# Even attention with its score tiles spread over the head, and its linear stages reordered

## The chip, the cores and the metric

The kernel runs on one core of one Trainium2 chip. The time is device microseconds for one execution, the median of three timed runs.

A core has five engines that run their own instruction queues side by side: TensorE (PE), which multiplies matrices and transposes; VectorE (DVE); ScalarE (ACT); GpSimd (POOL); and SyncE (SP), which here only starts DMAs. Results of PE go to PSUM, which has eight banks of 128 x 512 floats. PE's clock is either at its full level or at half of it; the profile gives the mean granted clock of a stretch as a share of the full one.

## What is computed

One step of a two-layer backbone on 128 prompt tokens and 512 sample tokens, all in 32-bit floats. Cut to what the change touches, the even layer is:

```
h   = rmsnorm(x) * (1 + scale) + shift
u   = h @ w_in                       # cq, ckv, kr, gate_a, q_b, k_b, v_b, gate_b
q   = rmsnorm(cq) @ w_uq             # 8 heads: 64 plain + 32 rotary columns
kv  = rmsnorm(ckv) @ w_ukv           # keys and values of the 8 MLA heads
o_a = softmax(q k^T) v * silu(gate_a)
o_b = softmax(q_b k_b^T) v_b * silu(gate_b)   # 8 heads, 2 key/value heads
x   = x + gate * (concat(o_a, o_b) @ w_out)
```

Sample tokens read 128 cached tokens and themselves (640 keys); prompt tokens read only the 128 prompt tokens. The odd layer has the same frame around an mLSTM (forward and backward, with a carried state) and a differential attention.

## The kernel before

Activations stand as 640 columns: 128 of the prompt, 512 of the sample. Nearly every product is computed as three passes over a high and a low part of both operands (`mm3`), the parts being made by a cast on ScalarE (`whi`, L76) and a subtraction (`wlo`, L77) for each weight piece. A scheduler orders each engine's instructions by a simulated timeline, with the order of the program as priority; within the even attention `pe_order` ties PE's instructions to the order in which the program issues them. `issue_after(x)` puts the instructions of a block behind x on x's engine.

**Linear stages of the even layer** (`even_linear`). Query lora and rotary key (e_wA), then ckv, k_b and v_b (e_wB), then the MLA queries in two halves (uq), values (ukvV, copied to `Va` by DVE at L559), keys (ukvK, copied to `kn` by ScalarE), and last q_b (e_wC) with its norm and rotation `evC` on DVE. Then `even_prep` lays out key tiles `Ka` and `kp`, the queries and keys of heads 0 and 1 are prepared, and `even_gates` multiplies the gates and applies silu (`silu_from`: a tanh on ScalarE, L127, and two DVE lines, L128 and L129, the second writing `og`).

**Even attention** (`attention`). Sixteen heads: 0 to 7 are the MLA heads, 8 to 15 the grouped ones. A head has four score tiles of 128 queries x 640 keys. `scores(h, i)` issues one: PE writes it into one of two score buffers (`s2`, two banks each); DVE takes the maximum (L628); ScalarE exponentiates it with the sum (L631); DVE inverts the sum (L634); GpSimd multiplies (L641). Three passes make an MLA tile, two a grouped one. `head_T(k)` transposes key block k of the head's four tiles (L648) into one of two `t1` banks, and ScalarE or DVE copies it to `pT` (L653, L651). `head_PV` multiplies the five blocks with the values, the value run (L659), into the one bank `o`; DVE multiplies that by the gate (L747). One iteration for head h issues, on PE, in this order: block 0 of h; tile 1 of h+1; block 1; tile 2; the transposes of the queries of h+2 (`prep[1]`, one call for two heads in the grouped part); block 2; tile 3; blocks 3 and 4; tile 0 of h+2; the value run of h; and `side(h)`, which holds the matmuls of the odd layer's modulation, later of the even gate. `prep[0]` casts the keys of h+2 (`kh` on DVE, L788) and subtracts (`kl` on GpSimd, L789). `split_psum` writes the query's upper part on ScalarE (L339) and the lower part on DVE (L340); in the grouped part these are L802 and L803.

The prompt's scores are computed four heads at a time by `prompt_quad`, in steps that `stage` advances: 0 prepares, 1 computes scores (L672) in a score buffer of `s2`, the maximum (L674), four exponentials `pp` (L678) and a product; 2 transposes; 3 multiplies with the values.

From head 12 on `op_load` fetches and splits output-projection weights (cast on ScalarE, subtraction on GpSimd), and in head 15 `ada_gate_row` sums the gate's parts, adds the bias (`grow`, L248) and sends the row to DRAM, from where `ada_gate_bc` reads it for the output projection.

**Odd layer.** `odd_linear` runs four projections (o_wK, o_wQ, o_wV1, o_wVM); `mlstm_gates`, a chain of scans on DVE with a few transposes, is issued after the first. In `mlstm_head`, for each of five blocks t, PE computes the value products `pv` (L1508) and then the product with the carried state `it`, which ScalarE scales into `nd` (L1518) and DVE adds (L1520). A `pacer` fills the gaps with matmuls of other projections, placed behind the instruction in `self.mark`.

Of the kernel before, what the change touches and what calls it, by code (L numbers as in the profile page):

```python
# [37 lines left out]
class K:  # L38
# [84 lines left out]
    def silu_from(self, out, src, shape, pool, other=None):  # L123

        nc = self.nc
# [4 lines left out]
        if other is not None:  # L130
            nc.vector.tensor_tensor(out=out, in0=out, in1=other, op=ALU.mult)
# [106 lines left out]
    def ada_gate_row(self, L, pool, tag, bufs):  # L238
# [103 lines left out]
    def even_linear(self, E, EM, H, L, ps):  # L342
# [198 lines left out]

        for hf in range(2):
# [11 lines left out]
        for t in range(6):  # L554
# [4 lines left out]
            nc.vector.tensor_copy(Va[:, t, :], acc)  # L559
# [12 lines left out]

        self.qb = E.tile([128, 5, 512], F32, tag="qb", name="qb", bufs=1)

        def evC(t, acc):
            q = self.qb[:, t]
            nc.scalar.copy(q, acc)
            qv = q.rearrange("p (h w) -> p h w", h=8)
            r = self.rsqrt(self.sumsq(q, 8, 64), 8, 64)
            nc.vector.tensor_tensor(out=qv, in0=qv, in1=r[:, :, None].to_broadcast([128, 8, 64]), op=ALU.mult)  # L580
            nc.vector.tensor_tensor(out=qv, in0=qv, in1=self.rows[:, None, R_GQ:R_GQ + 64].to_broadcast([128, 8, 64]),
                                    op=ALU.mult)
            if t:
                self.rope(qv, qv, *ropeB(t), 8, 64, L)

        self.lin_tok([(A["e_wC"][i], 2) for i in range(4)], 512, Hh, Hl, range(5), evC, ps)

# [3 lines left out]
    def even_gates(self, H, L, ps):  # L591
        Hh, Hl, A = self.Hh, self.Hl, self.A
        self.og = self.st.tile([128, 8, 640], F32, tag="ogx", name="og", bufs=1)
        for m in range(8):
            acc = self.lin_feat(A["e_wG"][m], Hh, Hl, ps)
            for j in range(2):
                self.silu_from(self.og[:, m, j * 320:j * 320 + 320], acc[j], [128, 320], L)
# [39 lines left out]
    def head_scores(self, T, ps, passes, i):  # L637
# [3 lines left out]
        self.nc.gpsimd.tensor_tensor(out=p, in0=p, in1=rs.to_broadcast([128, 640]), op=ALU.mult)  # L641
# [21 lines left out]
    def prompt_quad(self, T, ps, prep, V, cols, m):  # L663
# [4 lines left out]
        s = ps.tile([128, 2, 512], F32, tag="s2", name="sp", bufs=2)[:, 0]  # L668
# [1016 lines left out]
```

## Time and profile before

| | |
|---|---|
| median of three runs | 885.71 us (885.25 to 886.45) |
| the profiled execution | 888.68 us, its span 886.9 us |
| mean granted PE clock | 0.989 |
| busy of the span: PE, DVE, ACT, POOL | 839.8, 540.8, 416.9, 258.5 us |

The span runs from the first instruction to the last; the rest of an execution's time lies around it. The even layer's linear stages and gates take the span up to about 209 us, the even attention the stretch to 386.6, where the output projection begins. Busy times of the engines overlap, so they do not add up to the span. A busy PE is not a PE at its peak, since the profile models where a pipelined matmul ends. A wait is idle time of an engine before an instruction, put down to what released it.

### The profile page before, as it was taken

What the parts mean: (1) busy time and instruction counts of PE and PEld (TensorE: products, weight loads), DVE (VectorE), ACT (ScalarE), POOL (GpSimd) and SP (SyncE); (2) the same over time, 40 slices, a digit from 0 to 9 for tenths busy, and PEclk for the clock granted to TensorE, in tenths of its full rate; (3) what the DMA queues carried; (4) which work ended last, traced back from release to release, by engine and by line L of the source; (5) the groups of instructions that cost most, each with busy time, mean ns of one, the idle gap of its engine ahead of it and who ended that gap; (6) DMA issues with size and microseconds to landing.
All of it is one profiled execution on the core that took longest, in us unless ns stands there. A gap on an engine that the chain in (4) does not pass through costs nothing.

```text
span 886.9 us, 14375 instructions
## 1 busy us (share of the span) xinstructions
PE 839.8 (95%) x5418; PEld 715.7 (81%) x5418; DVE 540.8 (61%) x1174; ACT 416.9 (47%) x920; POOL 258.5 (29%) x240
## 2 busy tenths in 40 slices
PE   5999999998999999899999999999999899999996
PEld 2778988997787876668888788889989688888886
DVE  3574932973665777525662864277674846667755
ACT  5354533323566777624442234266554656443423
POOL 0010201522666576713230000322220834230121
PEclk9999999999999999999999999999999999999999
DMA  9821322221122211454203222222123222143303
GB/s 343 349 67 36 109 70 71 79 87 51 48 96 96 96 49 55 137 207 137 116 25 131 84 77 84 72 72 73 48 96 132 71 79 62 59 173 113 125 1 119
DMA packets 29642, 88.52 MB, mean 100 GB/s; under 512 B 3753, under 2 KB 6881, under 8 KB 29573
## 3 DMA queue, kind: packets, MB, share of 16 engines
q1 hardware_dynamic: 25904, 83.64, 27.6%
q10 hardware_dynamic: 3668, 3.96, 1.4%
q8 instruction: 43, 0.70, 0.3%
q14 instruction: 27, 0.21, 0.1%
HBM read 80.90 MB, written 6.68 MB: 99 GB/s over the span
## 4 chain that ended last, share of the span: by engine, by line
PE 82%; DVE 5%; ACT 4%; POOL 3%; DMA 3%; issue 2%; SPq 0%; POOLq 0%; ACTq 0%; DVEq 0%
PE acc L83 13%; PE acc L85 13%; PE acc L84 13%; PE s L621 7%; PE acc L120 6%; PE acc L1108 6%; PE o L659 4%; PE t L648 3%; PE pv L1508 2%; PE o L1194 2%; PE ada L190 2%; POOL p L641 1%; DMA adaw<-in_eada_ss_dram 1%; PE acc L569 1%; PE accA L85 1%
## 5 line engine op out<-in xcount | busy, mean ns | idle before, releaser
L84 PE MATMUL acc<-wlo,Hh 128*128 128x512 f32 (+2 forms) x400 | 149.5, 374 | 0.0
L85 PE MATMUL acc<-whi,Hl 128*128 128x512 f32 (+2 forms) x400 | 149.1, 373 | 0.2 <-DVE Hl L1006 0.2
L83 PE MATMUL acc<-whi,Hh 128*128 128x512 f32 (+2 forms) x400 | 146.6, 377 | 2.4 <-ACT Hh L1004 1.4
L77 DVE TENSOR_TENSOR wlo<-raw,whi 128x1024 fp32r<-128x1024 f32 (+4 forms) x67 | 81.5, 1218 | 92.7 <-ACT whi L76 92.0
L76 ACT CAST whi<-raw 128x1024 fp32r<-128x1024 f32 (+4 forms) x71 | 71.5, 1007 | 126.8 <-PE acc L85 90.0
L628 DVE TENSOR_REDUCE nm<-s 128x1 f32<-128x640 f32 (+1 forms) x104 | 81.1, 781 | 53.2 <-PE s L621 52.2
L641 POOL TENSOR_TENSOR p<-p,rs 128x640 f32<-128x640 f32 x64 | 79.9, 1263 | 69.5 <-DVE rs L634 38.5
L631 ACT ACTIVATE p<-s,nm 128x640 f32<-128x640 f32 (+1 forms) x104 | 79.5, 765 | 41.5 <-DVE nm L628 38.6
L48 POOL TENSOR_TENSOR rs_r<-rs_h,mhalf 128x1 f32<-128x1 f32 (+4 forms) x39 | 40.1, 1032 | 195.8 <-DVE rs_h L47 195.6
L83 PEld LDWEIGHTS acc<-whi,Hh 128*128 128x128 f32 x400 | 75.8, 190 | 15.0 <-ACT Hh L1004 1.7
L85 PEld LDWEIGHTS acc<-whi,Hl 128*128 128x128 f32 x400 | 76.0, 190 | 13.6 <-DVE Hl L1006 0.4
L84 PEld LDWEIGHTS acc<-wlo,Hh 128*128 128x128 f32 x400 | 76.1, 190 | 12.3
L648 PE MATMUL t<-cst,p 128*128 128x128 f32 x320 | 49.1, 282 | 5.8 <-POOL p L641 3.5
L85 PE MATMUL acc<-whi,ol 128*128 128x512 f32 (+1 forms) x124 | 48.0, 387 | 0.0
L83 PE MATMUL acc<-whi,oh 128*128 128x512 f32 (+1 forms) x124 | 47.1, 388 | 0.9 <-DVE grow L248 0.9
L84 PE MATMUL acc<-wlo,oh 128*128 128x512 f32 (+1 forms) x124 | 47.9, 388 | 0.0
L648 PEld LDWEIGHTS t<-cst,p 128*128 128x128 f32 x320 | 38.4, 144 | 10.7 <-POOL p L641 5.0
L653 ACT COPY pT<-t 128x512 f32<-128x512 f32 x56 | 32.2, 587 | 25.2 <-PE t L648 24.9
L634 DVE RECIPROCAL rs<-sm 128x1 f32<-128x1 f32 x104 | 16.6, 159 | 28.6 <-ACT p L631 27.8
L621 PE MATMUL s<-Kb,q 128*128 128x320 f32 x128 | 27.7, 339 | 5.7 <-ACT pp L678 3.2
L1108 PE MATMUL acc<-Hh,whi 128*128 128x320 f32 x128 | 32.5, 323 | 0.5 <-ACT v L1085 0.5
L120 PE MATMUL acc<-Hh,whi 128*128 128x320 f32 x128 | 32.7, 309 | 0.0
(384 smaller groups left out, 1923.0 us busy)
## 6 DMA issues: line engine op xcount, KB each, us to landing
adaw<-in_eada_ss_dram SPq DMA_DIRECT2D x16, 512.0 KB, 10.2
raw<-in_oada_ss_dram SPq DMA_DIRECT2D x16, 512.0 KB, 3.5
raw<-in_e_wG_dram SPq DMA_DIRECT2D x8, 512.0 KB, 3.6
raw<-in_eada_g_dram SPq DMA_DIRECT2D x8, 512.0 KB, 3.5
raw<-in_e_wO_dram SPq DMA_DIRECT2D x8, 512.0 KB, 3.5
raw<-in_oada_g_dram SPq DMA_DIRECT2D x8, 512.0 KB
raw<-in_o_wO_dram SPq DMA_DIRECT2D x8, 512.0 KB, 7.1
xT<-in_xT_dram SPq DMA_DIRECT2D x8, 320.0 KB, 5.7
```

The costliest lines, as they stand in the source:

```text
L76: (cp or nc.scalar.copy)(hi[:, 0:m], raw[:, 0:m])
L77: (lo_on or nc.vector).tensor_tensor(out=lo[:, 0:m], in0=raw[:, 0:m], in1=hi[:, 0:m], op=ALU.subtract)
L83: mm(out, lhsT=lh, rhs=rh, start=first, stop=False)
L84: mm(out, lhsT=lh, rhs=rl, start=False, stop=False)
L85: self.mark = mm(out, lhsT=ll, rhs=rh, start=False, stop=last)
L120: mm(acc[j][:, 0:320], lhsT=a[:, k], rhs=b[:, k, j * 320:j * 320 + 320], start=f, stop=l)
L621: self.mark = self.nc.tensor.matmul(out[:, j, 0:w], lhsT=q[0:rows, qcols], rhs=k[0:rows, a:a + w], start=i == 0, stop=i == len(passes) - 1)
L628: nc.vector.tensor_reduce(out=nm, in_=s, axis=AX.XY, op=ALU.max, negate=True)
L631: nc.scalar.activation(out=p[:, 0:n].rearrange("p (a b) -> p a b", a=s.shape[1]), in_=s, func=AF.Exp, bias=nm, accum_out=sm)
L641: self.nc.gpsimd.tensor_tensor(out=p, in0=p, in1=rs.to_broadcast([128, 640]), op=ALU.mult)
L648: self.nc.tensor.transpose(tp[:, i * 128:i * 128 + 128], p[i][:, k * 128:k * 128 + 128], self.ident)
L1108: nc.tensor.matmul(acc[j][:, 0:320], lhsT=a[:, k], rhs=b[:, k, j * 320:j * 320 + 320], start=f, stop=l)
```

## The change

- `silu_from` becomes `silu2`: (tanh + 1) * x in one DVE instruction, so `og` is doubled; `ada_gate_row` halves the even gate's row instead, in one more DVE instruction.
- q_b (e_wC, `evC`) is projected before the MLA queries; `Va`, the `Ka` and `kp` layouts and the first two heads' `kh` are copied by ScalarE instead of DVE.
- The score tiles of the next head are issued after block 0 (tile 2), after block 1 (tile 3), after block 3 (tile 0 of h+2), and behind the value run (tile 1 of h+2). The prompt's scores are written into the bank `o`, by a step that stands behind block 1.
- `prep[0]` is put behind the GpSimd product of the last tile issued (`self.pm`), and the second and third pass of an MLA score tile change places.
- `ada_gate_row("e")` moves ahead of the last head's value run.
- In the odd layer, `mlstm_gates` moves behind o_wV1, and in `mlstm_head` the product `it` moves ahead of `pv`, with the `mark` on the latter.

```diff
-    def silu_from(self, out, src, shape, pool, other=None):
+    def silu2(self, out, src, shape, pool):
         th = pool.tile(shape, F32, tag="th", name="th", bufs=2)
-        nc.scalar.activation(out=th, in_=src, func=AF.Tanh, scale=0.5)
-        nc.vector.tensor_scalar(out=th, in0=th, scalar1=0.5, scalar2=0.5, op0=ALU.mult, op1=ALU.add)
-        nc.vector.tensor_tensor(out=out, in0=th, in1=src, op=ALU.mult)
+        self.nc.scalar.activation(out=th, in_=src, func=AF.Tanh, scale=0.5)
+        self.nc.vector.scalar_tensor_tensor(out=out, in0=th, scalar=1.0, in1=src, op0=ALU.add, op1=ALU.mult)
...
         nc.vector.tensor_tensor(out=row, in0=ps[:, 0:256], in1=bias, op=ALU.add)
+        if L == "e":
+            nc.vector.tensor_scalar(out=row, in0=row, scalar1=0.5, scalar2=None, op0=ALU.mult)
...
-            nc.vector.tensor_copy(Va[:, t, :], acc)
+            nc.scalar.copy(Va[:, t, :], acc)
...
-        self.nc.gpsimd.tensor_tensor(out=p, in0=p, in1=rs.to_broadcast([128, 640]), op=ALU.mult)
+        self.pm = self.nc.gpsimd.tensor_tensor(out=p, in0=p, in1=rs.to_broadcast([128, 640]), op=ALU.mult)
...
-        s = ps.tile([128, 2, 512], F32, tag="s2", name="sp", bufs=2)[:, 0]
+        s = ps.tile([128, 512], F32, tag="o", name="sp", bufs=1)
...
         scores(1, 0)
+        scores(1, 1)
         rest = None
         for h in range(nh):
             p = [tiles.pop((h, i)) for i in range(4)]
             pt = [self.head_T(T, ps, p, 0, h)]
             if h + 2 < nh:
-                prep[0](h + 2, P)
-            scores(h + 1, 1)
+                with self.tc.issue_after(self.pm.ins):
+                    prep[0](h + 2, P)
+            scores(h + 1, 2)
             if rest:
                 rest()
             pt.append(self.head_T(T, ps, p, 1, h))
-            scores(h + 1, 2)
+            done = stage(1)
+            scores(h + 1, 3)
             if h + 2 < nh:
                 prep[1](h + 2, P)
-            pt.append(self.head_T(T, ps, p, 2, h))
-            scores(h + 1, 3)
-            pt += [self.head_T(T, ps, p, k, h) for k in (3, 4)]
+            pt += [self.head_T(T, ps, p, k, h) for k in (2, 3)]
             scores(h + 2, 0)
-            done = stage(0, 3)
+            pt.append(self.head_T(T, ps, p, 4, h))
+            done = done or stage(0, 3)
+            if h == nh - 1:
+                self.ada_gate_row("e", ps, "pr", 1)
             o = ps.tile([128, 512], F32, tag="o", name="o", bufs=1)
...
+            scores(h + 2, 1)
             rest = side(h)
-            if not done:
-                stage(1, 2)
+            done = done or stage(2)
...
-                nc.vector.tensor_copy(Ka[s][i][RR[s]], krT[i][:, 0:640])
+                nc.scalar.copy(Ka[s][i][RR[s]], krT[i][:, 0:640])
...
-            nc.vector.tensor_copy(kh[NR[e]], src)
+            (nc.scalar.copy if h < 2 else nc.vector.tensor_copy)(kh[NR[e]], src)
...
-            P[h] = [(qh, kh, KR[e]), (qh, kl, KR[e]), (ql, kh, KR[e])]
+            P[h] = [(qh, kh, KR[e]), (ql, kh, KR[e]), (qh, kl, KR[e])]
...
-            if r is None:
+            if nm == "o_wV1":
                 r = self.mlstm_gates(M, Gp, ps)
```

The moves of `evC` and of the product `it` are moves of whole blocks.

## Rows read from the trace of the kernel before

**Rows 1.** Busy time of an engine on the page's first part.

```profile
PE 839.8 (95%) x5418; PEld 715.7 (81%) x5418; DVE 540.8 (61%) x1174; ACT 416.9 (47%) x920; POOL 258.5 (29%) x240
```

**Rows 2.** Waits of PE, 208 to 388: total us, times, longest.

```profile
PE s L621 <- ACT pp L678: 4.2, 4, 2.7
PE t L648 <- POOL p L641: 3.5, 4, 2.1
PE s L621 <- ACT p L631: 2.5, 5, 1.0
PE t L648 <- ACT pT L653: 1.8, 4, 0.9
...
PE acc L83 <- DVE grow L248: 0.9, 1, 0.9
```

**Rows 3.** Windows: busy us (x count) of PE, PEld, DVE, ACT, POOL, PE's clock, DMA share, GB/s.

```profile
212.00:214.00 2.00, 2.00 (x16) 1.08 (x19) 1.45 (x3) 1.11 (x3) 0.06 (x1) 0.52 0.00 0
214.00:216.00 2.00, 2.00 (x14) 1.33 (x7) 0.16 (x1) 1.03 (x3) 2.00 (x2) 0.63 0.49 131
...
362.00:364.00 2.00, 2.00 (x10) 1.96 (x10) 0.99 (x2) 0.71 (x3) 2.00 (x3) 0.56 0.14 23
...
300.00:340.00 40.00, 37.32 (x322) 29.77 (x322) 30.18 (x64) 29.54 (x72) 27.39 (x23) 1.00 0.21 67
```

**Rows 4.** Timeline at 209: start, us, engine, line, out<-in, count, idle before.

```profile
209.44 0.65 DVE L128 TENSOR_SCALAR th<-th 128x320 f32<-128x320 f32 x2 [5.59 <-ACT th L127]
...
210.55 0.85 PE L621 MATMUL s<-Ka,qh 96*128 96x320 f32 x4 [1.47 <-DVE og L129]
```

**Rows 5.** Timeline of GpSimd and PE at the first transposes.

```profile
218.67 1.54 POOL L789 TENSOR_TENSOR Ka<-kn,Ka 64x640 fp32r<-64x640 f32 x1 [2.26 <-DVE rs L634]
...
220.17 3.67 POOL L641 TENSOR_TENSOR p<-p,rs 128x640 f32<-128x640 f32 x3
...
221.47 0.33 PE L648 MATMUL t<-cst,p 128*128 128x128 f32 x1 [2.10 <-POOL p L641]
222.68 0.48 PE L648 MATMUL t<-cst,p 128*128 128x128 f32 x1 [0.88 <-POOL p L641]
```

**Rows 6.** Timeline of ScalarE and PE at the longest wait, 359 to 362.

```profile
359.29 1.04 ACT L76 CAST whi<-raw 128x1024 fp32r<-128x1024 f32 x1 [0.62 <-DMA raw<-in_e_wO_dram]
...
361.62 0.80 ACT L631 ACTIVATE p<-s,nm 128x640 f32<-128x640 f32 x1
...
361.79 1.07 PE L621 MATMUL s<-Kb,q 128*128 128x320 f32 x4 [2.72 <-ACT pp L678]
```

**Rows 7.** Timeline of an MLA head's query, PE and DVE.

```profile
249.34 0.60 PE L810 MATMUL qtp<-cst,qa 128*128 128x128 f32 x4
...
250.47 0.67 DVE L651 COPY pT<-t 128x512 f32<-128x512 f32 x1
251.06 0.68 DVE L340 TENSOR_TENSOR ql<-qtp,qh 128x512 fp32r<-128x512 f32 x1
...
251.12 1.03 PE L648 MATMUL t<-cst,p 128*128 128x128 f32 x8
251.91 0.83 PE L621 MATMUL s<-Ka,qh 96*128 96x320 f32 x4
```

**Rows 8.** Timeline of a grouped head's query.

```profile
329.63 0.60 PE L798 MATMUL qtp<-cst,qb 128*128 128x128 f32 x4
...
331.19 0.68 DVE L803 TENSOR_TENSOR q<-qtp,q 64x512 fp32r<-64x512 f32 x1
```

**Rows 9.** Timeline where the output projection begins.

```profile
386.59 0.50 PE L83 MATMUL acc<-whi,oh 128*128 128x512 f32 x1 [0.86 <-DVE grow L248]
```

**Rows 10.** Windows, columns as in Rows 3: evC's stretch and the odd projections.

```profile
160.00:180.00 20.00, 20.00 (x138) 20.00 (x137) 19.27 (x42) 7.07 (x13) 7.61 (x6) 1.00 0.25 80
...
520.00:560.00 40.00, 40.00 (x239) 35.68 (x238) 19.86 (x33) 14.76 (x29) 2.17 (x3) 1.00 0.26 86
```

**Rows 11.** Waits of PE, 686 to 790.

```profile
PE pv L1508 <- DVE nd L1520: 0.5, 1, 0.5
```

More of the change, by code (lines that the diff above doesn't have):

```diff
@@ L539, in even_linear, with evC @@
         self.lin_tok([(A["e_wB"][i], 2) for i in range(4)], 512, Hh, Hl, (1, 2, 3, 4, 0), evB, ps)
+        self.qb = E.tile([128, 5, 512], F32, tag="qb", name="qb", bufs=1)
+        def evC(t, acc):
+            q = self.qb[:, t]
+            nc.scalar.copy(q, acc)
+            qv = q.rearrange("p (h w) -> p h w", h=8)
+            r = self.rsqrt(self.sumsq(q, 8, 64), 8, 64)
+            nc.vector.tensor_tensor(out=qv, in0=qv, in1=r[:, :, None].to_broadcast([128, 8, 64]), op=ALU.mult)
+            nc.vector.tensor_tensor(out=qv, in0=qv, in1=self.rows[:, None, R_GQ:R_GQ + 64].to_broadcast([128, 8, 64]),
+                                    op=ALU.mult)
+            if t:
+                self.rope(qv, qv, *ropeB(t), 8, 64, L)
+        self.lin_tok([(A["e_wC"][i], 2) for i in range(4)], 512, Hh, Hl, range(5), evC, ps)
         for hf in range(2):
@@ L570, in even_linear @@
                 nc.scalar.copy(kn[:, m, c], acc[:, 0:384])
[L573 to L586, printed above, removed]
         self.Hh, self.Hl = Hh, Hl
@@ L1502, in mlstm_head @@
         for t in range(5):
-            acc = ps.tile([128, 512], F32, tag="pv", name="pv", bufs=1)
-            for d in range(2):
-                js = [0] if t == 0 else (list(range(1, t + 1)) if d == 0 else list(range(t, 5)))
-                for i, j in enumerate(js):
-                    s, lo = sm[d][j]
-                    nc.tensor.matmul(acc[:, d * 129:d * 129 + 129], lhsT=s[:, t * 128 - lo:t * 128 - lo + 128],
-                                     rhs=v1[:, j, h], start=i == 0, stop=i == len(js) - 1)
-            av = acc[:, 0:258].rearrange("p (d v) -> p d v", d=2)
-            if t == 0:
-                nc.vector.tensor_copy(nd[:, t], av)
-            else:
+            if t:
                 it = ps.tile([128, 512], F32, tag="it", name="it", bufs=1)
@@ L1519, in mlstm_head @@
                                          scale=wi[:, t, col[d]:col[d] + 1])
+            acc = ps.tile([128, 512], F32, tag="pv", name="pv", bufs=1)
+            for d in range(2):
+                js = [0] if t == 0 else (list(range(1, t + 1)) if d == 0 else list(range(t, 5)))
+                for i, j in enumerate(js):
+                    s, lo = sm[d][j]
+                    self.mark = nc.tensor.matmul(acc[:, d * 129:d * 129 + 129],
+                                                 lhsT=s[:, t * 128 - lo:t * 128 - lo + 128],
+                                                 rhs=v1[:, j, h], start=i == 0, stop=i == len(js) - 1)
+            av = acc[:, 0:258].rearrange("p (d v) -> p d v", d=2)
+            if t == 0:
+                nc.vector.tensor_copy(nd[:, t], av)
+            else:
                 nc.vector.tensor_tensor(out=nd[:, t], in0=av, in1=nd[:, t], op=ALU.add)
```

9 lines of the change are left out of this document (2 added, 7 removed).

## The prediction

> **What bounds the kernel now.** I read the page's first part first: the matrix engine (PE) is busy for 95% of the span [rows 1]. The change takes no matmul away, so a gain can only come out of the 5% in which PE waits and out of the stretches in which its clock is low. I then asked for PE's waits in the stretch of the even attention, 208 to 388 us, in which nearly all lines of the change lie [rows 2]. The reader is to see five waits there: 4.2 us of score tiles that wait for the exponentials of the prompt scores (pp), 3.5 us of transposes that wait for GpSimd's multiplication of p, 2.5 us of score tiles that wait for their own exponentials, 1.8 us on copies of pT, and at the stage's end 0.9 us on the gate row (grow). Ahead of them stands a wait of 1.47 us for the last gate product (og) [rows 4]. Last, the windows of 2 us [rows 3]: after the first, the second and the largest of these waits the granted clock falls to its lower level for part of 4 us (0.52 and 0.63 of full speed from 212 to 216, 0.56 from 362 to 364). There are three such falls in the stage, the second from 222 to 226, and each costs about (0.48 + 0.37) x 2 = 1.7 us. So the stage holds some 14 us of named waits and 5 us of low clock; that is all that can be won there.
>
> **What the change takes away.** *The last gate product.* Two DVE lines per half become one. The first scores, at 210.55, wait for L129, which stands behind both halves' L128: 0.65 us from 209.44 [rows 4]. With L128 gone its successor starts at 209.44 and not at some 210.0. I take 0.5 us (between 0, if the fused line costs as much as the two, and 0.5).
>
> *The opening.* The first transposes waited 2.10 us and then 0.88. GpSimd runs the key subtraction (L789, 1.54 us) between the p products of the first two tiles and those of the last two [rows 5]. The change puts that subtraction behind the product of tile (1,1), and it puts the scores of that tile, some 0.9 us of PE work, into the gap. Of 2.98 us I take 2.0 (between 1.0, if the exponential of tile (0,3) frees the score bank late, and 3.0). In every later head the subtraction stands behind a product too, and the products of the next two tiles queue behind it. It is wanted by the third pass of a score tile some 4 us after the head's first transposes, while the product and the subtraction take 1.2 + 1.54: nothing; without that cover, up to 1.5 us in each of six heads.
>
> *The prompt scores.* They leave the score banks for the bank of the value run, so score tiles no longer wait for pp: 4.2 us in four waits, 2.7 of them in one [rows 2]. But that one is not only pp. ScalarE stood [rows 6] at the cast of a weight that had not landed (0.62 us), cast it in 1.04 us, and only then came the four prompt exponentials (the 1.29 us up to 361.62) and the tile's own. The first two stay. I take 3.0 (between 1.5 and 4.2). In exchange the value run must wait until pp has been read. Between them lie a score tile, two transposed blocks, a score tile and one more block: 0.83, 0.79, 0.83 and 0.4 us of PE work by rows 7, against some 0.7 us for the maximum (DVE's 0.67 and 0.68 for as many columns there) and 1.3 for the exponentials, so I cost this wait at nothing; without that cover it would be 2.0 us in each of four heads.
>
> *Spreading the score tiles.* Before, three of a head's four tiles stood close together among the transposes, and a tile may start only when the one two before it has been exponentiated. With one behind the value run the distances even out: I take all 2.5 us of those waits (between 0.5 and 2.5). The 1.8 us on pT copies I leave as they are.
>
> *The clock falls.* The second should go with the opening's waits; the third stands behind the 2.72 us wait, and I give it one chance in two: 1.5 falls, 2.6 us (between 0 and 5.1).
>
> *The end.* The gate row's matmuls now stand ahead of the last value run, whose ten matmuls hide the addition that the output projection waited 0.86 us for [rows 9]. With a little of the last transposes' wait I take 1.0 (between 0.4 and 1.3). The moved step issues a bias load and four stores on SyncE's queue; the last weight load for the projection may end up behind the stores. It is wanted only in the second half of the projection's first pass, and the extra halving of the row lies in the same cover: nothing; without the cover, the 0.86 us of now and some 0.4 for the halving.
>
> Sum of the gains: 0.5 + 2.0 + 3.0 + 2.5 + 2.6 + 1.0 = 11.6 us; by the bounds, 3.4 and 16.6.
>
> **What it adds.** The new order brings the first score tile of head h+2 close behind the transposes of its queries. Before: query transposes, a block of transposes, a score tile, two blocks, then that tile. After: query transposes, two blocks, then that tile. The two blocks, eight transposes, take 0.79 us (251.12 to 251.91 in rows 7), so four query transposes take 0.4. The query itself takes longer: its transposes start at 249.34 and end at about 249.75, and its lower half (L340) ends at 251.74, 2.0 us later, because DVE copies a pT (L651) ahead of it. In the MLA heads the lower half is now wanted by the second of three passes (the change swaps the last two), about 1.1 us after the transposes. So PE waits 0.9 us if DVE keeps its order, and 0.3 if the subtraction goes ahead of the copy; I take 0.6, six times. In the grouped heads both halves are needed at once: the transposes end at about 330.05, the lower half at 331.87 [rows 8], 1.8 us against 0.8: I take 1.0 four times (0.6 if both engines are free). Everything behind it in PE's fixed order, the last block, the value run and the next scores, waits with it. Sum 3.6 + 4.0 = 7.6 us. If all is short it is 4.2. In the four heads with prompt scores the four exponentials may stand ahead of the query's cast, 1.3 us more each: with the long values 5.4 + 4.0 + 5.2 = 14.6.
>
> **What is moved elsewhere.** The query projection (e_wC) goes ahead of three smaller ones, and its DVE work (norm and rotation) now runs beside their weight splits in place of the gates'. In the stretch where it ran before, DVE was 96% busy and PE still lost nothing [rows 10], so: 0. The smaller projections take their weights faster, so up to +1.5; the copies that go to ScalarE may give 0.5 back. In the odd layer the mLSTM gates move behind a later projection. DVE there is half idle (19.86 of 40 us in rows 10), 0, up to +1.0 if their chain reaches the differential attention. The interior product of a head now stands ahead of the value run, so its scaling on ScalarE runs beside the matmuls; PE waited for the sum of the two for 0.5 us [rows 11]: -0.5 (up to 0).
>
> **The sum.** -11.6 + 7.6 - 0.5 = -4.5 us. The profiled execution took 888.68 us, of which the span is 886.9, so it becomes 884.2. The median of the three timed runs is 885.71, 3.0 less than the profiled one; with the same distance I predict 881.2. About 0.2%, 1.8 us, is what can be told from no change here.
>
> **The rivals.** *The queries hide.* If ScalarE and DVE take the query before the pT copies, and the low clock goes from the opening altogether (the gap at 209 shrinks by a third), the gains come to some 15 and the cost to 4.2: -11.3, 874.4. For it: both engines are idle for a quarter of the grouped heads (30.18 and 29.54 us busy of 40 in rows 3), and their order is made anew. Against it: [rows 7] show an order that serves the copy first.
>
> *The queries decide (slower).* The place is the first score tile of the head after next, in ten heads. With gains of 11.6 it decides from 1.2 us a time. At the long bound of 14.6 us, and with the clock falls left as they are (gains 9.0), the time is +5.6 - 0.5, 890.8. For it: the grouped heads already show 1.8 us against 0.8. Against it: while PE waits there, the other chains catch up, so part of the wait only replaces one that was there.
>
> *The low clock spreads (slower too).* Short waits that come in every head could pull the clock down again and again: ten falls of 1.7 us would be +17, 898. The Trainium skill, "TensorE: Matmul & The Clock Gate", section "A second HAM failure mode: psum-queue depth-cycling", says that a matrix engine which idles briefly but often between groups of matmuls goes back and forth between its two clock levels. By that rule this change would be a loss. The trace disagrees: from 300 to 340 us, with the 1.0 us wait of rows 2 and several shorter ones, the granted clock is 1.00 [rows 3]. I give it little.
>
> *The waits only move.* PE's order is written out, so an engine that is late is waited for somewhere; if costs and gains are equal the time stays within 885.7 +- 1.8.
>
> **How the numbers follow.** Forecast, 876 to 884: 0.42. Queries hide, below 876: 0.26. Only moved: 0.12. Queries decide: 0.17. Low clock spreads: 0.03. So faster 0.68, same 0.12, slower 0.20. The predicted time is the forecast's, 881. The range leaves out the best corner of the bounds and the spread of low clock: 871 to 890. The forecast's own range is 876 to 884.
>
> **What would show it.** Right: no score tile waits for pp; the key subtraction runs after the fourth p product or later; the projection starts without a wait for grow; a new wait of a score tile for the query's lower half (DVE L340 and L803 of now) in ten heads, 0.5 to 1 us each; one or two low stretches in place of three between 208 and 388 us; the linear stages as long as before. Wrong: if those query waits are missing, the gain is over 8 us; if they reach 1.2 us, or if the value run waits for pp, there is no gain.

## The result, and the profile after

The changed kernel takes 893.83 us (median of five runs, 891.9 to 894.54), the kernel before beside it 886.45 us: ratio 1.0075, with a 95% interval of 1.0055 to 1.0095. It is slower by 7.4 us. The forecast was 4.5 us faster. The profiled execution has a span of 892.8 us, 5.9 more than before.

Where the 5.9 us come from is read by cutting both spans at the first score tile and at the end of the last value run. Up to the first score, 210.5 us became 205.6; the even attention, 174.6 us, became 190.3; what is behind it, 501.7 us, became 496.9. So everything but the attention got shorter, by 9.7 us, and the attention lost 15.7. (Single marks carry some us of scatter. Ahead of the first score, the trace of before has a stretch of low clock at 20.9 us, which takes 1.7 us of full clock, and a wait of 2.5 us for a transfer; the changed kernel's trace has neither, but E6 and E14 below have such a stretch and E3 a wait of 2.0. With the changed linear stages the first score comes at 205.6 to 209.7.) One window over the attention of each kernel divides that loss (columns as in [rows 3]); first before, then after:

```profile
210.55:385.16 174.61, 160.96 (x1376) 128.41 (x1380) 111.21 (x238) 111.12 (x262) 109.88 (x85) 0.97 0.26 85
```

```profile
205.57:395.90 190.33, 168.13 (x1381) 129.44 (x1381) 116.88 (x240) 110.03 (x262) 110.15 (x85) 0.96 0.24 79
```

PE's idle time, the length less the busy time, went from 13.7 to 22.2 us. Its busy time grew by 7.2 us, for five matmuls more (four of the gate row, one of the projection). So more than half of the loss is waiting, and most of the rest is the same work done more slowly.

**The waits.** PE's waits of the changed kernel from 200 to 400 us, as in [rows 2]:

```profile
PE s L619 <- DVE ql L338: 7.7, 6, 1.9
PE s L619 <- DVE q L805: 7.3, 4, 3.1
PE s L619 <- ACT p L629: 3.0, 4, 1.1
...
PE s L619 <- ACT qh L337: 1.1, 2, 0.6
...
PE t L646 <- POOL p L639: 0.4, 1, 0.4
```

The reader is to see what is missing and what is new. The waits for pp (4.2 us) are gone, those for GpSimd's product fell from 3.5 to 0.4 us, grow is gone. The first two rows and the fourth of those shown were not there before: score tiles that wait for a query, 16.1 us in ten heads. Each is the first tile of head h+2, as foretold; the price is over twice the 7.6 us that were set for it.

**Why the query is late in an MLA head.** The timeline of PE, POOL, ScalarE and DVE around one such tile (the changed kernel; start, length):

```profile
261.40 1.55 POOL L791 TENSOR_TENSOR Ka<-kn,Ka 64x640 fp32r<-64x640 f32 x1
...
261.72 1.58 DVE L790 CAST Ka<-kn 64x640 fp32r<-64x640 f32 x1 [0.41 <-PE s L619]
261.74 0.60 PE L812 MATMUL qtp<-cst,qa 128*128 128x128 f32 x4
...
262.38 0.59 ACT L337 CAST qh<-qtp 128x512 fp32r<-128x512 f32 x1
...
263.23 0.81 DVE L626 TENSOR_REDUCE nm<-s 128x1 f32<-128x640 f32 x1
...
264.03 0.66 DVE L649 COPY pT<-t 128x512 f32<-128x512 f32 x1
...
264.62 0.67 DVE L338 TENSOR_TENSOR ql<-qtp,qh 128x512 fp32r<-128x512 f32 x1
...
265.35 0.56 PE L619 MATMUL s<-Ka,ql 128*128 128x320 f32 x2 [1.77 <-DVE ql L338]
```

From the query's transposes to the end of its lower half it is 3.55 us (261.74 to 265.29), where the kernel before took 2.4 (249.34 to 251.74, [rows 7]). On DVE three instructions stand between the transposes and it: the key cast of a later head, a maximum and a pT copy. In the kernel before, no key cast stood there, and the maximum was over (250.35) before ScalarE had made the query's upper half (250.56); only the copy stood behind that:

```profile
249.53 0.82 DVE L628 TENSOR_REDUCE nm<-s 128x1 f32<-128x640 f32 x1 [0.63 <-PE s L621]
...
249.97 0.59 ACT L339 CAST qh<-qtp 128x512 fp32r<-128x512 f32 x1
```

The key cast, which took 0.47 to 0.49 us in five of its six places before, takes 1.58 beside GpSimd's key subtraction (E5 tests that). There are three such long casts, 1.61, 1.46 and 1.58 us (at 233.14, 247.40 and 261.72), and behind them come the three longest waits of the MLA heads, 1.79, 1.90 and 1.77.

**Why it is late in a grouped head.** The worst place, in the iteration of head 12:

```profile
358.38 1.04 ACT L76 CAST whi<-raw 128x1024 fp32r<-128x1024 f32 x1 [0.80 <-DMA raw<-in_e_wO_dram]
...
359.33 0.36 ACT L676 ACTIVATE pp<-sp,nm 128x128 f32<-128x128 f32 x1
...
360.71 0.58 ACT L804 CAST q<-qtp 64x512 fp32r<-64x512 f32 x1
...
361.32 0.68 DVE L805 TENSOR_TENSOR q<-qtp,q 64x512 fp32r<-64x512 f32 x1 [0.28 <-ACT q L804]
...
362.06 1.43 PE L619 MATMUL s<-Kb,q 128*128 128x320 f32 x4 [3.11 <-DVE q L805]
...
363.29 1.05 PE L646 MATMUL t<-cst,p 128*128 128x128 f32 x4
...
364.27 4.13 PE L657 MATMUL o<-pT,Vb 128*64 128x256 f32 x20
```

This is the old longest wait [rows 6] under another name: the weight that has not landed, its cast and the four prompt exponentials still stand ahead on ScalarE, and now the query's cast stands behind them, too. PE waits 3.11 us in place of 2.72.

**The clock.** Windows of 2 us of the changed kernel, columns as in [rows 3]:

```profile
224.00:226.00 2.00, 2.00 (x13) 1.12 (x13) 0.84 (x2) 1.39 (x3) 0.78 (x1) 0.63 0.00 0
...
238.00:240.00 2.00, 2.00 (x11) 1.17 (x12) 0.68 (x2) 1.39 (x3) 0.29 (x2) 0.54 0.00 0
...
252.00:254.00 2.00, 2.00 (x15) 1.66 (x15) 0.82 (x1) 0.99 (x2) 0.56 (x1) 0.50 0.03 8
...
364.00:366.00 2.00, 2.00 (x10) 1.01 (x10) 1.14 (x3) 1.37 (x3) 0.21 (x1) 0.50 0.29 117
```

There are four falls to the lower level (1.2 in place of 2.4 GHz), where there were three. Added up over the attention, 2 us x (1 - granted clock), they take 8.5 us of full clock, before 5.1. Three begin 0.7 to 1.6 us behind the end of a query wait (1.45 us, over at 222.96; 1.79, at 236.80; 1.90, at 251.15); the fourth, twice as long as the others, begins within the wait of 3.11 us that is over at 362.06. What lies right behind such a tile in the new order is a block of transposes and the whole value run. The run just shown took 4.13 us, one in E3, whose trace has no fall in the attention, 2.38. By line and form, the changed kernel's value run and then that of E3:

```profile
L657 PE MATMUL o<-pT,Va 128*64 128x256 f32 x160 | 23.0, 445 | 0.0
L657 PE MATMUL o<-pT,Vb 128*64 128x256 f32 x160 | 20.7, 409 | 0.0
```

```profile
L657 PE MATMUL o<-pT,Vb 128*64 128x256 f32 x160 | 19.1, 383 | 0.0
L657 PE MATMUL o<-pT,Va 128*64 128x256 f32 x160 | 18.9, 383 | 0.0
```

That is 5.7 us (5.9 against the kernel before, where both rows have 18.9), the greater part of the 7.2 us by which PE's busy time grew.

**What went as foretold.** The gate product and the opening:

```profile
205.57 0.56 PE L619 MATMUL s<-Ka,qh 96*128 96x320 f32 x2 [0.90 <-DVE og L127]
...
213.34 0.56 PE L619 MATMUL s<-Ka,qh 128*128 128x320 f32 x2 [0.67 <-ACT p L629]
...
215.22 0.33 PE L646 MATMUL t<-cst,p 128*128 128x128 f32 x1 [0.40 <-POOL p L639]
```

The first wait fell by 0.57 us [rows 4], the opening's two from 2.98 us [rows 5] to 1.07.

### The profile page after: what moved, and what is told of

Its sections match the earlier page's. It is cut to its first block, busy times and chain, and to the rows that moved or that the text cites. A ratio compares the mean times of both kernels' runs of the same rounds, so it can differ in the third digit from the quotient of the medians.

```text
span 892.8 us, 14356 instructions
## 1 busy us (share of the span) xinstructions
PE 843.3 (94%) x5418; PEld 716.6 (80%) x5418; DVE 535.0 (60%) x1143; ACT 424.8 (48%) x936; POOL 250.7 (28%) x240
## 4 chain that ended last, share of the span: by engine, by line
PE 80%; DVE 8%; ACT 3%; issue 3%; DMA 3%; POOL 2%; SPq 1%; POOLq 0%; ACTq 0%; DVEq 0%
PE acc L83 13%; PE acc L85 12%; PE acc L84 12%; PE s L619 7%; PE acc L120 6%; PE acc L1108 6%; PE o L657 5%; PE t L646 3%; PE pv L1515 2%; PE o L1194 2%; DVE nm L626 1%; PE ada L186 1%; PE gps L230 1%; PE acc L583 1%; DMA raw<-in_o_wO_dram 1%
## 5 line engine op out<-in xcount | busy, mean ns | idle before, releaser
L83 PEld LDWEIGHTS acc<-whi,Hh 128*128 128x128 f32 x400 | 75.5, 190 | 14.6 <-ACT Hh L1004 1.7
L85 PEld LDWEIGHTS acc<-whi,Hl 128*128 128x128 f32 x400 | 76.0, 190 | 13.5 <-DVE Hl L1006 0.4
L48 POOL TENSOR_TENSOR rs_r<-rs_h,mhalf 128x1 f32<-128x1 f32 (+4 forms) x39 | 36.9, 951 | 148.0 <-DVE rs_h L47 147.7
L619 PE MATMUL s<-Ka,qh 96*128 96x320 f32 (+1 forms) x128 | 31.9, 332 | 2.8 <-ACT qh L337 1.1
L1108 PE MATMUL acc<-Hh,whi 128*128 128x320 f32 x128 | 32.5, 323 | 0.5 <-ACT v L1085 0.5
```

Source lines behind the costliest of these rows:

```text
L83: mm(out, lhsT=lh, rhs=rh, start=first, stop=False)
L85: self.mark = mm(out, lhsT=ll, rhs=rh, start=False, stop=last)
L619: self.mark = self.nc.tensor.matmul(out[:, j, 0:w], lhsT=q[0:rows, qcols], rhs=k[0:rows, a:a + w], start=i == 0, stop=i == len(passes) - 1)
L1108: nc.tensor.matmul(acc[j][:, 0:320], lhsT=a[:, k], rhs=b[:, k, j * 320:j * 320 + 320], start=f, stop=l)
```

## The experiments

The theory from these rows: the distance between the query's transposes and their first score tile is too short, and the falls of the clock that follow these waits double their price. The rivals: the prompt's scores in the value bank cost it; the linear part disturbs the attention; DVE and ScalarE are late as a whole, so that any cure only renames the wait. Diffs are against the changed kernel unless said otherwise. The columns of the table: ratio to the kernel before on the same chip with its 95% interval; then, from one profiled execution, the length of the even attention, PE's idle time in it, the part of that which is score tiles waiting for a query, and falls of the clock with the full clock lost. (One execution need not be the usual one: the profiled one is the slowest of the changed kernel's five, of E9's six and of E12's twelve, and the fastest of E13's twelve.)

| | median us | ratio | attention us | idle us | query waits us | falls, us lost |
|---|---|---|---|---|---|---|
| before | | 1 | 174.6 | 13.7 | 0 | 3, 5.1 |
| changed | 893.83 | 1.0075 (1.0055 to 1.0095) | 190.3 | 22.2 | 16.1 | 4, 8.5 |
| E1 | 881.14 | 0.9950 (0.9929 to 0.9972) | 172.9 | 13.4 | 0 | 2, 3.4 |
| E2 | 897.18 | 1.0144 (1.0109 to 1.0178) | 187.6 | 22.2 | 16.1 | 3, 5.1 |
| E3 | 880.54 | 0.9943 (0.9927 to 0.9959) | 176.9 | 15.9 | 8.2 | 0, 0 |
| E4 | 894.58 | 1.0098 (1.0080 to 1.0116) | 191.5 | 22.2 | 14.3 | 5, 8.5 |
| E5 | 885.49 | 0.9995 (0.9980 to 1.0010) | 182.3 | 18.6 | 12.1 | 2, 3.4 |
| E6 | 887.71 | 1.0024 (1.0008 to 1.0041) | 184.0 | 19.6 | 13.0 | 2, 3.4 |
| E7 | 883.41 | 0.9981 (0.9967 to 0.9995) | 178.9 | 16.5 | 0 | 1, 1.7 |
| E8 | 885.48 | 1.0002 (0.9985 to 1.0019) | 182.4 | 18.2 | 0 | 2, 3.4 |
| E9 | 880.37 | 0.9941 (0.9922 to 0.9959) | 178.5 | 15.8 | 7.3 | 1, 1.7 |
| E10 | 882.12 | 0.9960 (0.9943 to 0.9976) | 177.8 | 15.2 | 6.4 | 1, 1.7 |
| E11 | 880.28 | 0.9941 (0.9920 to 0.9963) | 172.8 | 14.5 | 0.7 | 1, 1.7 |
| E12 | 883.80 | 0.9984 (0.9965 to 1.0003) | 185.3 | 18.8 | 12.6 | 2, 6.8 |
| E13 | 883.79 | 0.9994 (0.9981 to 1.0007) | 179.2 | 18.8 | 11.0 | 0, 0 |
| E14 | 888.86 | 1.0051 (1.0034 to 1.0068) | 185.2 | 19.3 | 12.9 | 3, 5.1 |
| E15 | 881.81 | 0.9969 (0.9950 to 0.9988) | 175.2 | 13.7 | 1.9 | 2, 5.1 |
| E16 | 885.53 | 1.0023 (1.0002 to 1.0045) | 182.4 | 18.6 | 12.6 | 2, 3.4 |
| E17 | 884.50 | 1.0001 (0.9986 to 1.0017) | 179.3 | 19.0 | 0 | 1, 3.4 |
| E18 | 880.06 | 0.9939 (0.9920 to 0.9958) | 173.6 | 13.5 | 2.2 | 2, 3.4 |

**E1, E2: the attention and the rest, each alone.** E1 is the changed kernel with `prompt_quad`, `attention`, `even_prep` and `even_attention` as before; E2 is the kernel before with these four as changed.

> The changed kernel with the old even attention (order, score bank of the prompt, key copies, pass order); its linear stages, fused gates and odd layer stay changed. Theory (the loss lies in the attention alone, +14.2 us there, while the other stages gained 2.3 + 1.0 + 2.2 + 0.1 = 5.6): 886.4 - 5.6, so 880 to 882, and the even attention lasts 176 us (175 to 178). Rival (the linear part disturbs the attention, by the clock or by the state of the queues it leaves): the attention lasts over 182 us and the time stays above 886.

> The kernel before with the new even attention alone. Theory: 893.8 + 5.6 = 899, 897 to 901, the attention lasts 189 to 192 us, and the waits of score tiles for the query's lower half in it come to 14 to 18 us, as in the changed kernel (16.1). Rival (the parts disturb each other): below 892.

As the theory said: the loss is the attention's, 1.0075 / 0.9950 = 1.0126 or 11 us, and E2's 1.4% over the kernel before agrees. The attention was shorter than expected in both (172.9 and 187.6 us). The rest of the change is worth 0.5% (E1), or 0.7% (E2 against the changed kernel).

**E3: the queries earlier.**

```diff
             done = stage(1)
-            scores(h + 1, 3)
             if h + 2 < nh:
                 prep[1](h + 2, P)
+            scores(h + 1, 3)
```

> The changed kernel with the query transposes of head h+2 moved one score tile earlier, ahead of tile 3 of h+1 (some 0.8 to 1.3 us of PE work more between them and the tile that wants them). Theory (the query waits and the clock falls behind them are the loss): the query waits fall from 16.1 to under 5 us, one or more of the falls at 224, 240, 252 and 362 go, the attention lasts 170 to 180 us and the time is 877 to 884. Rival (DVE and ScalarE as a whole are too late, the queries are only where it shows): the wait moves to p, pT or another tile, the attention stays over 186 us, and the time is above 889.

One line moved takes 13 us off and turns a loss of 0.75% into a gain of 0.57%. The query waits fell less than expected (8.2 and not under 5), but the trace has no fall of the clock in the whole attention; E3's five runs have a mean granted clock of 0.997 to 0.999, the changed kernel's 0.987 to 0.991. The rival of engines late as a whole falls. That the longer distance alone did it is not shown: what else the move changed is told behind E10.

**E4: the prompt's scores back in a score buffer.** `s = ps.tile([128, 2, 512], F32, tag="s2", name="sp", bufs=2)[:, 0]`, as before.

> The changed kernel with the prompt's scores in a score buffer again, as before. Theory (the value bank is not the cause): the waits for pp come back, 3 to 5 us in four heads, and the query waits stay; 895 to 899. Rival (the prompt scores in the value bank hold up the value run or push the query's cast back): the time falls to below 890.

No score tile waits for pp here either, and one wait of the prompt's own scores, 1.9 us, is new. The time is the changed kernel's within the interval: the bank is not the cause, and it did not bring the 3 us, either.

**E5, E6: what stands ahead on DVE.** E5 takes the hold on the keys away, E6 puts their cast on ScalarE:

```diff
# E5
-                with self.tc.issue_after(self.pm.ins):
-                    prep[0](h + 2, P)
+                prep[0](h + 2, P)
# E6
-            (nc.scalar.copy if h < 2 else nc.vector.tensor_copy)(kh[NR[e]], src)
+            nc.scalar.copy(kh[NR[e]], src)
```

> The changed kernel with the key cast and subtraction of head h+2 no longer held behind the product of the last tile. In the changed kernel DVE's key cast (1.58 us at 261.72) stands ahead of the query's lower half and runs at the same time as GpSimd's key subtraction (1.55 us at 261.40), while it took 0.49 us when GpSimd multiplied p in the kernel before. Theory (that overlap is a part of the query waits of the MLA heads): the cast goes back to 0.5 to 0.7 us, the MLA query waits fall from 7.7 us to 3 to 5, the opening's wait of some 2 us comes back, the grouped heads stay at 7.3; 887 to 893. Rival (the cast is only a neighbour): MLA query waits stay at 7 to 8 and the time is 894 to 897.

> The changed kernel with the key casts of all MLA heads on ScalarE. DVE then has 0.5 to 1.6 us less ahead of the query's lower half. Theory: MLA query waits fall from 7.7 us to under 5 and one or two of the clock falls at 224, 238 and 252 go; 886 to 891. Rival (ScalarE, which also casts the query and exponentiates, is as late as DVE was): the wait changes its name to the query's upper half, and the time is 892 to 896.

E5 wins 0.8%, more than expected, with an edit that leaves PE's order alone. The six key casts by line and form, in the changed kernel and then in E5:

```profile
L790 DVE CAST Ka<-kn 64x640 fp32r<-64x640 f32 x6 | 6.7, 1111 | 1.5 <-PE s L619 1.4
```

```profile
L789 DVE CAST Ka<-kn 64x640 fp32r<-64x640 f32 x6 | 3.8, 632 | 1.3 <-PE s L619 1.2
```

The hold moved GpSimd's subtraction to just the time in which DVE casts the next key. The cast that starts at 261.72, behind a subtraction that runs to 262.95, ends 0.35 us after it; at 233.14 and 247.40 it ends 0.34 and 0.36 us after it. So by these rows DVE does not slow down, it stands until GpSimd is done. The expectation's explanation of the short casts was wrong, though: in the kernel before, GpSimd began its product just behind the start of the cast, and it was the product that took longer, 1.49 us in place of 1.25:

```profile
252.57 0.49 DVE L788 CAST Ka<-kn 64x640 fp32r<-64x640 f32 x1
...
252.68 1.49 POOL L641 TENSOR_TENSOR p<-p,rs 128x640 f32<-128x640 f32 x1 [0.73 <-DVE rs L634]
```

The one cast there that started beside a running product, at 229.98, took 0.93 and ended 0.36 us after it. The Trainium skill, "SBUF — State Buffer", section "Who interferes with whom", says that a VectorE cast can need the port pair that it shares with GpSimd, and that then whichever starts second is blocked until the first has finished; these rows agree. The MLA waits for `ql` went to 4.1 us (the three of 1.79, 1.90 and 1.77 to 0.60, 0.86 and 0.60), the falls from four to two, and the opening lost only 0.5 us (0.4 to 0.9). E6 says the same from the other side: waits for `ql` 1.4 us, but for ScalarE's `qh` 4.4.

**E7, E8: more cover still.** E7 is E3 with block 4 ahead of `scores(h + 2, 0)`; E8 is the changed kernel with `scores(h + 2, 0)` behind the value run, just ahead of `scores(h + 2, 1)`.

> The kernel with the query transposes ahead of tile 3 (880.5), and also block 4 ahead of tile 0 of head h+2: 0.4 us of PE work more between the query and its tile. Theory (what is left of the query waits, 8.2 us in ten heads, is still cover that lacks): 10 x 0.4 = 4 us less, minus up to 1 us of waits of block 4's copy, 876 to 879. Rival (DVE and ScalarE are late as a whole, the wait moves on): 880 to 882, with as much in waits for p or pT.

> The changed kernel with tile 0 of head h+2 behind the value run, beside tile 1: 0.4 + 2.3 us more PE work between the query and its tile, and the value run no longer stands behind the wait. Theory (the loss is the query wait, and the half clock in which the value run then stands: 445 and 409 ns a matmul in place of 383): query waits under 2 us, value run back at 383, no fall behind the query; the new waits are for the copies of pT ahead of the value run and, for tile 1, for the exponential of tile 3, 0.2 to 0.5 us a head; 878 to 886. Rival (spreading is what matters): two tiles side by side cost as much as the queries did, 890 or more.

Both take the query waits to nothing, and neither is better than E3; E7 is slower than both of its ranges. PE's waits in E7:

```profile
PE t L646 <- ACT pT L651: 8.5, 14, 1.7
PE t L646 <- DVE pT L649: 3.0, 3, 1.5
```

Three blocks in a row outrun the two `t1` banks. Here the rival was right: beyond some point the wait only changes its name. In E8 it is 11.9 us for pT copies and 4.1 for exponentials.

**E9, E10: both cures, and the old order of the passes with them.** E9 is E3 with E5's edit; E10 is E9 with `[(qh, kh, KR[e]), (qh, kl, KR[e]), (ql, kh, KR[e])]`.

> The changed kernel with both cures at once: the queries ahead of tile 3 (alone 880.5) and the keys not held back (alone 885.5). Theory (the two sides of one wait: how early the query is transposed, and what DVE does before its lower half): the MLA query waits fall from 4.1 us to under 2, the opening loses some 0.5, no clock fall or one; 876 to 881. Rival (with the queries early enough the key cast no longer matters): 880 to 883.

> As the one before, with the old order of the passes in the MLA heads (the query's lower half wanted by the third pass and not by the second, 0.3 us later). Theory: what is left of the MLA query waits goes, 0 to 1.5 us less than the one before. Rival (the second pass now waits for the key's lower half): 0 to 2 us more.

The cures do not add up. E10 is E9 within the intervals.

The key casts by line and form in E3, and then in E12 (below), say why:

```profile
L790 DVE CAST Ka<-kn 64x640 fp32r<-64x640 f32 x6 | 4.7, 778 | 0.6 <-PE s L619 0.5
```

```profile
L790 DVE CAST Ka<-kn 64x640 fp32r<-64x640 f32 x6 | 3.4, 574 | 0.1
```

In both the hold on the keys stands as it was, and still the three long casts are down to 0.49 to 0.65 us: there they start where GpSimd's subtraction has some 0.3 us left or less. The runs that keep the long casts, E2, E4 and E14, have 8.8 to 9.3 us of query waits in the MLA heads, as the changed kernel has (8.9); the runs that lose them and still wait for queries there (E3, E5, E6, E9, E10, E12, E13, E16) have 2.5 to 5.9. So in these heads most of the cure is the end of that collision, whichever edit brings it: E5, which leaves the distance alone, takes the waits (for `ql` and `qh`) to 5.2 us, E3 to 4.1.

**E12: the old order of the passes alone** (E10's line in the changed kernel).

> The changed kernel with the old order of the passes in the MLA heads alone. Theory (the lower half comes late, when it is wanted matters by one pass of 0.3 us in six heads): MLA query waits 7.7 - 1.8 = 6, falls as before or one fewer: 888 to 893. Rival (the key's lower half, held back behind a product, is then waited for by the second pass): 893 to 897.

Much more than expected: 0.9% for one pass of 0.3 us in six heads. The query waits fell by 3.5 us, a third of the gain, and not by the pass alone, since the long key casts are gone as well. Much of the rest is the clock, as its twelve runs show. Time against mean granted clock of the whole execution, runs of the same kernel with the same clock averaged:

| clock | before (12 runs, beside E1 to E4) | changed | E12 |
|---|---|---|---|
| 0.987 | | 894.5 | |
| 0.989 | 887.7 | 894.0 | 889.7 |
| 0.991 | 886.3 | 892.1 | |
| 0.993 | 885.5 | | 887.4 |
| 0.995 | 883.8 | | 884.6 |
| 0.999 | | | 882.3 |

(E12's three runs at 0.994, 0.996 and 0.997 took 885.6, 883.6 and 884.0.) Each of these kernels takes 0.6 to 0.8 us more for each 0.001 less of clock, and most of its scatter goes with that; in E2 it is 1.1. How much low clock an execution meets differs from run to run. Over their runs the clock is 0.9894 in the changed kernel and 0.9957 in E12; 0.0063 x 0.7 is 4.4 us of their 10. At one clock, 0.989, they differ by 4.3 us (two runs against one). Before and after differ by 5.8 us at 0.991 (six runs against two), and the remaining 1.6 of 7.4 goes with the clock.

**E11, E15, E18: the old order with parts of the new.** E11 is E1 with the prompt's scores in the bank `o` (`stage(1)` behind block 1, `stage(2)` at the end) and the gate row ahead of the last value run. E15 holds the keys of head 2 alone back; E18 adds `scores(1, 1)` ahead of the loop.

> The old order of the even attention (881.1 beside the changed linear stages and odd layer), with the prompt's scores in the value bank, computed behind block 1, and the gate row ahead of the last value run. Theory (these two steps were right by themselves): the waits for pp, 4.6 us, fall to under 1.5 and the 0.9 us wait for grow goes, with them perhaps the clock fall at 358; 874 to 878. Rival (pp's exponentials stand ahead of the query's cast, and the wait becomes one for the query or for p): 880 to 883.

> The old order with the prompt's scores in the value bank (880.3), with the keys of head 2 alone held behind the product of the last tile. Theory (the opening's subtraction costs the old order 2.3 + 0.9 us of waits, and the fall at 220 stands behind them): the first wait falls under 1 us, the fall goes, 880.3 - 2 - 1.4 = 877, 875.5 to 879. Rival (the wait is for the exponential or the products themselves): 879.5 to 881.

> The old order with the prompt's scores in the value bank and the keys of head 2 held back, and tile (1,1) ahead of the first transposes, as in the changed kernel. Theory: of the opening's 1.9 us of waits 0.5 to 1 stay, the long fall behind them (four windows of 0.5) goes: 881.8 - 1 - 2.5 = 878, 876 to 880. Rival (the fall comes in the next waits): 881 to 882.

E11 equals E1 (0.9941 against 0.9950). The wait for pp, 4.6 us in E1, is gone; PE's waits in E11 show where it is:

```profile
PE s L619 <- ACT p L629: 4.6, 7, 1.7
PE t L646 <- POOL p L639: 4.2, 4, 2.3
PE t L646 <- DVE pT L649: 3.2, 3, 1.1
```

In E1 these were 2.4, 3.8 and 0 us. E15 missed: the opening's wait is shorter (1.06 and 0.83 us at the first transposes, not 2.31 and 0.88), but its fall is longer; its twelve runs stand in two groups, six at a clock of 0.987 to 0.989 (883.6 to 885.6 us) and six at 0.995 to 0.997 (878.6 to 880.0). E18 is the fastest of all by its median, 0.61% faster than before, and equal to E1, E3, E9 and E11 within the intervals. The four runs in the old order (E1, E11, E15, E18) also have DVE copy the key layouts, as before, and PE waits 1.9 us for a query's lower half ahead of the first score; in the runs where ScalarE copies them that wait is not there. The old order with ScalarE's copies was not run.

**E13, E14, E16: the cures by heads.** E13 moves only the MLA queries (`h < 6`) ahead of tile 3, E14 only the grouped ones; E16 holds the keys back for `h == 0` alone.

> The changed kernel with the queries ahead of tile 3 in the MLA heads alone. Each fall of the clock costs some 1.4 us (over the runs of one kernel the time rises by 0.75 us for each 0.001 of mean granted clock, and a fall is 0.0019 of it). Theory (waits and falls add up by place): MLA query waits 7.7 to 4.1, the falls at 224, 238 and 252 go, the grouped heads keep 7.3 us and the fall at 360: 893.8 - 3.6 - 4.2 = 886, 884 to 888. Rival (the falls are drawn by something else than the query waits): two or more falls stay before 300 us, 889 to 891.

> The changed kernel with the queries ahead of tile 3 in the grouped heads alone. Theory: grouped query waits 7.3 to 4.1, the fall at 360 goes, the MLA heads keep 7.7 us and three falls: 893.8 - 3.2 - 1.4 = 889, 887 to 891; both parts together give the 13.3 us that both at once gave. Rival (the parts don't add up): below 885 or above 893.

> The changed kernel with the keys held back in the opening alone, and free in the other five MLA heads. Theory (holding back paid 0.5 us in the opening and cost some 8 us in the heads behind it): the opening's wait is 0.4 us as in the changed kernel, the MLA query waits 3.5 to 5, 884 to 886. Rival (what costs is the first held subtraction, which shifts all that follow): 890 to 894.

Against the changed kernel E13 wins 0.81%, E14 0.24%, together 1.05% where E3 won 1.32%; with intervals of some 0.2% on each, they add up within the noise. Of what the two win, three quarters lies in the MLA heads. E13's trace also says something of the falls: its longest query wait is nearly the changed kernel's, a value run stands right behind it, and the clock stays at 1.00 from 352 to 364 us:

```profile
353.45 0.85 PE L619 MATMUL s<-Kb,q 128*128 128x320 f32 x4 [2.83 <-DVE q L807]
354.14 0.60 PE L646 MATMUL t<-cst,p 128*128 128x128 f32 x4
354.67 2.38 PE L657 MATMUL o<-pT,Vb 128*64 128x256 f32 x20
```

E6 has the like, 3.02 us at 359.98. E16 is the like of E5 (1.0023 against 0.9995, the intervals overlap a little): most of the hold's cost comes from the five heads behind the opening.

**E17: the queries earlier than in E3.** Modulation matmuls (`side`) ahead of tile 1, their second half ahead of tile 2, the queries ahead of block 1.

> The kernel with the queries ahead of tile 3 (880.5), with the modulation matmuls ahead of tile 1, their second half ahead of tile 2, and the queries behind tile 2, ahead of block 1: 0.4 us more cover, and the query no longer waits for the modulation's sum (1.7 us in five waits). Theory: query waits 8.2 to 4 to 5 us, 880.5 - 4 - 1.5 = 875, 873.5 to 878. Rival (the early half of the modulation waits for its copy on ScalarE, 0.3 to 0.6 us in seven heads, and the query's wait moves to p): 879 to 882.

Slower than both ranges, in the way of the rival: no query waits, and 3.6 us for the key's lower half, which GpSimd now finishes last, 6.6 for exponentials, 4.7 for pT.

## Why the prediction was wrong, step by step

**The step that failed** is "What it adds". Mechanism and place were right, the first score tile of head h+2 in ten heads. The size was not: 0.6 us in the MLA heads, where 8.8 / 6 = 1.5 us were measured, and 1.0 in the grouped ones, where it was 7.3 / 4 = 1.8; 16.1 us against 7.6, more than the long bound of 14.6. The MLA term took its length of 2.0 us from a row in which DVE had only one copy left to do when the query's upper half was made. In three of the six heads of the new order a long key cast, a maximum and the copy all stood there; without the long casts, in E5, the six waits come to 5.2 us, 0.9 each. The cast comes from a step that was costed at nothing, the hold on the key subtraction: the working asked when the subtraction's result is wanted, and not what GpSimd would run beside. E5 and E16 show that as much as 0.5 to 0.8% hung on it. The bound of the grouped term let the prompt exponentials stand ahead of the query's cast; they did at head 12, and with them the weight cast and its wait, which were left where they were.

**The clock falls** were to go from three to one and a half, a gain of 2.6 us. There were four, one of them double, and they fell on the value run. The rival "queries decide" named the outcome (890.8, with the point of decision at 1.2 us each). That its time comes within 3.0 us is in part luck: the query waits were 1.5 us longer than its 14.6 and the clock lost 3.4 us more than before, gains that it counted did not come, and the stages outside the attention gave back more than it had. The range ended at 890, while the bounds of the working, gains of 3.4 and a cost of 14.6, reach to 896. The rival "low clock spreads" was dismissed on a stretch without falls. The rule that stood beside it, of a matrix engine that idles briefly and often (the Trainium skill, "TensorE: Matmul & The Clock Gate", section "A second HAM failure mode: psum-queue depth-cycling"), came nearer than the text allowed, in four heads and not in ten; but E3, with ten query waits of 0.3 to 1.8 us, has no fall at all. Which wait brings a fall is not settled: 1.45 us at 222.96 was followed by one, 1.77 us at 265.35 was not, nor were 1.75 us in E3, 2.83 in E13 and 3.02 in E6; and E7 and E8 have falls without any query wait.

**Prompt scores, 3.0 us, and spreading, 2.5 us**, were not real gains. The waits for pp went to nothing, as foretold, but E4 and E11 show no time for it: what PE no longer waits for there it waits for a little later. The waits for the exponentials, which spreading was to end, rose from 2.5 to 3.0 us.

**Right:** the last gate product (0.5, measured 0.57), the opening (2.0, measured 1.9, of which the hold on the keys brought 0.5), the end (1.0, measured 1.4; the wait for grow is gone). The value run waits for no pp. **Moved elsewhere** was too cautious: 0.5 us was expected, and behind the attention alone the span is 4.8 us shorter, 1.4 of which is the end (projection 1.43 us behind the last value matmul before, at once after). E2, with the new attention and the old odd layer, is shorter there by the same 1.4 us (500.4 against 501.7), so the other 3.5 came with the odd layer's two moves, which were not tried one by one. That the linear stages stayed as long as before, the last sign named, the marks can't tell: the first score came 4.9 us earlier, but a low stretch and a transfer wait, together of about that size, come and go ahead of it.

**What stays open.** E3's attention has 2.5 us more of idle PE than E1's (15.9 against 13.4), and no falls, where E1's has two. Their times are equal through the clock: on the same chip E3's five runs stand at 0.997 to 0.999 and E1's seven at 0.989 to 0.997, and at 0.997, where each has two, E3 takes 881.1 and 881.3 us and E1 878.7 and 879.1. So at equal clock the spread order is the slower one even with its queries early, by some 2 us on these four runs. Whether it avoids falls by itself, or by the luck of where its waits lie, these runs don't tell; no version beat 0.9939 (E18).

## What to carry to other kernels

When a load or a preparation is moved nearer to its use, price it by what the new order puts ahead of it on each engine that makes it, not by its length in the old trace; and ask of each instruction that is held back what it will then run beside. Where PE's order is fixed, a wait can be paid twice if a long run of matmuls stands right behind it, since a fall of the clock may land there; compare kernels at the same mean granted clock before a difference is put down to waits. A wait that is removed is a gain only if the whole kernel's time says so: of the 16 us of query waits here, the first 8, with the clock falls that went along, were worth 13 (E3), and the other 8 nothing (E7). And a cure need not work for the reason it was chosen: ask whether it also moved what runs side by side.

## What the runs showed of the hardware

- A DVE cast of 64 x 640 that starts well within a GpSimd instruction ends 0.34 to 0.36 us after GpSimd does, and so took up to 1.61 us in the changed kernel and 2.54 in E17, behind two GpSimd instructions in a row; started first, it took 0.47 to 0.49. ScalarE's casts of the same keys take 0.71 to 0.73 us, with GpSimd at work or not (E6).
- Runs of one kernel differ by up to 10 us, mostly in step with the granted clock: E2 from 894.1 us at 0.995 to 904.2 at 0.986, E16 from 883.4 at 0.997 to 892.2 at 0.987, E12 from 881.9 at 0.999 to 889.7 at 0.989.
- A wait of PE of 2.83 us (E13) or 3.02 (E6) just ahead of a value run brought no fall of the clock; one of 1.45 us (changed kernel) was followed by one.
